# Prompt attention of a hybrid decoder layer: TensorE's order written out by hand, with transposes and value products three steps behind the scores

## The chip, the cores and the metric

The kernel runs on one core of a Trainium2 chip. The metric is the device time of one execution, in microseconds (us). The core has TensorE (PE in the profile: matmuls, with its weight loads, PEld, as a row of their own), VectorE (DVE), ScalarE (ACT), GpSimd (POOL), SyncE (SP, which issues most DMAs here) and the DMA engines. Each engine works through its own instructions in order and waits on semaphores for the others.

## What is computed

The reference is one inference step of a decoder layer over a prompt (2048 tokens) and a group of samples (8 x 8 tokens). Half of the mixing width is softmax attention over three strided windows, merged by their denominators; the other half is an RWKV-7 mixing, and an MLP follows. The change concerns the prompt's attention alone, which the reference states thus (8 heads of 64, blocks of 128 queries):

```python
BRANCHES = ((128, 1), (512, 4), (2048, 16))
...
    for w, d, M, N, band, bias in statics:
        ...
        s = jnp.einsum('bmrhe,bnrhe->bhrmn', qr, kr).astype(f32) * scale + bias[None, :, None]
        ...
        mx = jnp.max(s, -1)
        e = jnp.exp(s - mx[..., None])
        dn = jnp.sum(e, -1)
        o = jnp.einsum('bhrmn,bnrhe->bhrme', e, vr.astype(f32))
    ...
    for mx, dn, o in zip(maxs, dens, outs):
        sc = jnp.exp(mx - mall)
        num = num + sc[..., None] * o
        den = den + sc * dn
    return num / den[..., None]
```

## The kernel before

The program is one long list of stages: norms and the input projection, RWKV mixing, the prompt's attention, the samples' attention, the output projection, the MLP. A tile scheduler takes the instructions as the Python code emits them, chooses an order on each engine, and sets the semaphores. Where the code doesn't fix an order, the scheduler is free to put an instruction earlier or later on its engine than it was emitted.

The prompt's attention works on pairs of heads, p = 0 to 3 (`attention(p, pump, ahead)`), and in each pair on the branches b = 0, 1, 2 and four groups of queries. A group is two steps in b = 0 and 1 and one step in b = 2, so a pair has 8 + 8 + 4 = 20 steps. A step does this for each of the two heads (`ty`):

- scores `sc`: queries against keys, the keys in a high and a low part (`kst`, `klo`). Both heads together are 8 matmuls in b = 0 and 1, nearly all of 256 columns, and 16 of 128 columns in b = 2. The queries `qst` are read in steps of 1, 4 and 16 elements in the three branches.
- on VectorE one operation per block of scores that adds the bias (`bt`) and takes the maximum into `st`, and on ScalarE an exponential into `e`, with its sum into `st`.
- four transposes of `e` into `pt`, which `evac` copies into `pts`: every other copy on ScalarE, the others on VectorE.
- eight value products `o` out of `pts` and the values `vt`; after the last step of a group ScalarE copies `o` into `ob`.

When a pair is through, `merge(p)` is made. It is a generator, and `pump()` moves it on by two of its `yield`s after each step of the next pair. It takes maxima and denominators out of `st` (GpSimd into `zst` and `mv2`, 40 and 8 small matmuls into `sw`), works out a weight for each branch on VectorE and ScalarE (`nall`, `scw`, `dn`, `wh`), stores it (`wD`) and loads it back in another layout (`wrow`); both DMAs go through SP. Twelve matmuls of `wrow` with `wsel` then spread the weights, VectorE multiplies `ob` by them, and GpSimd adds the branches up (VectorE in the last pair, where the merge has no next pair to lie in). The output projection (`pwo`), whose weights `wo` ScalarE and VectorE split out of `raw` at the end of the stage, follows behind the last merge.

Buffers: `e` four, `pts` four, `pt` two, `sc` three, `o` two, `ax` (the merge's, pairs 0 to 2) one, `vt` four.

Of the kernel before, what the change touches and what calls it, by code (L numbers as in the profile page):

```python
# [9 lines left out]
F32 = mybir.dt.float32  # L10
# [161 lines left out]
def _build(ctx, tc, nc, I, O, dbg, upto):  # L172
# [879 lines left out]

    def attention(p, pump, ahead):
# [5 lines left out]
        for b in range(3):  # L1059
# [7 lines left out]
            vt = None  # L1067
            for grp in range(4):
                vp, vt = vt, next_v()
                o = ppo.tile([P, 512], F32, name="o")  # L1070
                for t2 in range(0, 4, 2 if b < 2 else 4):
                    tl = [grp * 4 + t2 + i for i in range(2 if b < 2 else 4)]
                    w = 512 // len(tl)
                    work = []
                    for ty in range(2):
                        kst, klo, qst = K[ty]
                        ps = psc.tile([P, 512], F32, name="sc")
                        e = ae.tile([P, 512], F32, name="e", bufs=4)
                        blocks = []
                        for x, i in enumerate(tl):  # L1080
# [3 lines left out]
                            PE.matmul(ps[:, c0:c0 + n], cols(qst, b, i, False), cols(kst, b, i, both), start=True, stop=False)  # L1084
                            PE.matmul(ps[:, c0:c0 + n], cols(qst, b, i, False), cols(klo, b, i, both), start=False, stop=True)  # L1085
# [3 lines left out]
                            for hb in range(n // P):  # L1089
                                old = n // P - 1 - hb  # L1090
                                if b == 0:
                                    kv = vt[:, i % 4 - old] if i % 4 >= old else vp[:, 3]
                                else:
                                    kv = (vp if old else vt)[:, i % 4]
                                blocks.append((i, kv, c0 + hb * P, hb == 0, hb == n // P - 1))
                        work.append((e, blocks))
                    ptss = []
                    for e, blocks in work:
                        pt = ppt.tile([P, 512], F32, name="pt")
                        pts = at.tile([P, 512], F32, name="pts", bufs=4)  # L1100
                        for y, (i, kv, c0, fst, lst) in enumerate(blocks):
                            PE.transpose(pt[:, y * P:(y + 1) * P], e[:, c0:c0 + P], ident)  # L1102
                        nb = len(blocks)
                        evac(pts[:, :nb * P], pt[:, :nb * P])
                        ptss.append(pts)
                    for y in range(nb):
# [567 lines left out]
```

## Time and profile before

| | us |
|---|---|
| three runs, median (lowest to highest) | 3356.25 (3349.73 to 3358.73) |
| the profiled execution, its own time | 3357.47 |
| its span, first to last instruction | 3355.7 |
| TensorE busy in the span | 3135.5 (93%) |
| TensorE's weight loads busy | 2865.0 (85%) |
| VectorE busy | 2157.2 (64%) |
| ScalarE busy | 1469.2 (44%) |
| GpSimd busy | 976.1 (29%) |
| first score of the prompt's attention | 1207.76 |
| first matmul of the output projection | 1623.21 |

Busy time is the sum of an engine's instructions, without its waits; a share close to 100% over the whole span doesn't say that the engine bounds each stage, so stages are read from windows of the trace. Matmuls overlap in the trace: each row has a start and a modelled end, and the next one starts before that end.

### The profile page before, as it was taken

Reading aid. Unit: us, or ns where it says so; the run is one execution under the profiler, and the core shown is the slowest. Engines: PE = TensorE matmul, PEld = TensorE weight load, DVE = VectorE, ACT = ScalarE, POOL = GpSimd, SP = SyncE. Lnnn points to the kernel's source line nnn. Section 1 sums busy time; section 2 is a strip of 40 time slices with the busy share of each in tenths; the row PEclk is TensorE's granted clock in tenths of the full one; section 3 lists DMA queues with packets and bytes.
Section 4 is the critical chain, followed back from the end, with each engine's and each line's share of the span. In section 5 each row is a group of like instructions: output and inputs, shape, how many; then the busy total and the mean of one; then the engine's idle time right before and its main releaser. Section 6 shows DMA issues by size and latency. Waiting matters only on the chain.

```text
span 3355.7 us, 63761 instructions
## 1 busy us (share of the span) xinstructions
PE 3135.5 (93%) x24214; PEld 2865.0 (85%) x24214; DVE 2157.2 (64%) x4547; ACT 1469.2 (44%) x3497; POOL 976.1 (29%) x1141
## 2 busy tenths in 40 slices
PE   5999899989988979999799689999999999999999
PEld 5876877877787868888688579999899999899999
DVE  4656677677566435656554577676976767967675
ACT  4545566555555446677222233232433323433332
POOL 1003422453044100111000233343533334533332
PEclk9999999999998989999899789999999999999999
DMA  5465575466456383323766322222232222222222
GB/s 169 137 185 149 131 204 158 109 157 178 124 131 178 106 279 117 126 74 90 243 221 235 123 85 89 64 85 64 98 113 64 88 63 86 88 68 84 64 89 73
DMA packets 349144, 418.55 MB, mean 125 GB/s; under 512 B 117252, under 2 KB 210367, under 8 KB 348837
## 3 DMA queue, kind: packets, MB, share of 16 engines
q1 hardware_dynamic: 348836, 414.48, 41.6%
q8 instruction: 190, 3.11, 0.4%
q14 instruction: 118, 0.96, 0.1%
HBM read 325.62 MB, written 93.46 MB: 125 GB/s over the span
## 4 chain that ended last, share of the span: by engine, by line
PE 72%; DMA 9%; DVE 9%; SPq 3%; issue 2%; POOL 2%; ACT 2%; DVEq 0%; POOLq 0%; ACTq 0%
PE pm L1603 20%; PE pm L1557 17%; PE pj L334 7%; PE pwo L1451 5%; PE pj L802 4%; PE o L1109 3%; PE pt L1102 2%; PE sc L1084 2%; PE sc L1085 2%; DVE ml L182 2%; DMA wr<-in_wq 1%; DMA wr<-in_wr 1%; DVE rl L1517 1%; DVE wl L1477 1%; DMA xg<-in_xg 1%
## 5 line engine op out<-in xcount | busy, mean ns | idle before, releaser
L185 ACT ACTIVATE wh<-wr 128x512 fp32r<-128x512 f32 x744 | 463.4, 625 | 818.5 <-PE pm L1603 473.4
L1603 PE MATMUL pm<-fh,wl 128*128 128x352 f32 x1536 | 495.9, 323 | 8.8 <-DVE wl L1477 8.8
L1603 PE MATMUL pm<-fh,wh 128*128 128x352 f32 x1536 | 493.4, 324 | 0.0
L1603 PE MATMUL pm<-fl,wh 128*128 128x352 f32 x1536 | 492.6, 323 | 0.5 <-DVE fl L182 0.5
L1557 PE MATMUL pm<-ml,wh 128*128 128x352 f32 x1344 | 437.0, 325 | 15.1 <-DVE ml L182 15.1
L1557 PE MATMUL pm<-mh,wh 128*128 128x352 f32 x1344 | 438.6, 327 | 9.4 <-ACT mh L185 9.2
L1557 PE MATMUL pm<-mh,wl 128*128 128x352 f32 x1344 | 436.0, 325 | 5.7 <-DVE wl L1477 4.6
L182 DVE TENSOR_TENSOR res<-pm,res 128x352 f32<-128x352 f32 x384 | 198.6, 522 | 287.5 <-PE pm L1603 284.7
L1477 DVE TENSOR_TENSOR wl<-wr,wh 128x512 fp32r<-128x512 f32 x432 | 361.1, 836 | 6.1 <-ACT wh L185 3.5
L1603 PEld LDWEIGHTS pm<-fh,wl 128*128 128x128 f32 x1536 | 290.2, 189 | 9.8 <-DVE wl L1477 9.8
L1603 PEld LDWEIGHTS pm<-fl,wh 128*128 128x128 f32 x1536 | 289.4, 189 | 1.3 <-DVE fl L182 1.1
L1603 PEld LDWEIGHTS pm<-fh,wh 128*128 128x128 f32 x1536 | 289.2, 189 | 0.8 <-ACT fh L185 0.2
L1557 PEld LDWEIGHTS pm<-ml,wh 128*128 128x128 f32 x1344 | 256.5, 191 | 19.1 <-DVE ml L182 19.0
L1557 PEld LDWEIGHTS pm<-mh,wh 128*128 128x128 f32 x1344 | 256.2, 191 | 11.5 <-ACT mh L185 11.5
L1557 PEld LDWEIGHTS pm<-mh,wl 128*128 128x128 f32 x1344 | 255.8, 190 | 8.9 <-DVE wl L1477 7.3
L802 PE MATMUL pj<-wh,nh 128*128 128x256 f32 (+1 forms) x816 | 242.4, 298 | 13.5 <-ACT qn L185 6.7
L802 PE MATMUL pj<-wh,nl 128*128 128x256 f32 (+1 forms) x816 | 241.1, 296 | 2.2 <-DVE nl L182 2.2
L334 PE MATMUL pj<-nh,wh 128*128 128x512 f32 (+3 forms) x600 | 222.8, 374 | 20.4 <-ACT nh L185 10.4
L1481 POOL TENSOR_TENSOR wr<-wr 128x512 f32<-128x512 f32 x48 | 68.9, 1435 | 591.0 <-DVE wl L1477 502.6
L802 PE MATMUL pj<-wl,nh 128*128 128x256 f32 (+1 forms) x816 | 240.7, 296 | 0.0
L182 DVE TENSOR_TENSOR wl<-wr,wh 128x512 fp32r<-128x512 f32 (+1 forms) x216 | 150.2, 698 | 135.2 <-ACT wh L185 130.0
L334 PE MATMUL pj<-nl,wh 128*128 128x512 f32 (+3 forms) x600 | 222.0, 371 | 5.9 <-DVE nl L182 5.9
(312 smaller groups left out, 7262.2 us busy)
## 6 DMA issues: line engine op xcount, KB each, us to landing
wr<-in_w SPq DMA_DIRECT2D x384, 256.0 KB
wr<-in_wr SPq DMA_DIRECT2D x120, 256.0 KB
wr<-in_wq SPq DMA_DIRECT2D x96, 256.0 KB
kv<-in_kc SPq DMA_DIRECT2D x40, 512.0 KB
kv<-in_vc SPq DMA_DIRECT2D x40, 512.0 KB
xsD<-xst SPq DMA_DIRECT2D x56, 256.0 KB
xrkv<-xsD SPq DMA_DIRECT2D x32, 384.0 KB
vt<-vD SPq DMA_DIRECT2D x48, 256.0 KB
```

The source lines that it names most:

```text
L182: V.tensor_tensor(out, a, b, op)
L185: S.activation(out, in_, func, bias=bias, scale=scale, **kw)
L334: PE.matmul(ps[:m, :n], a[:, k, :m], b[h * 4 + k][:, c0:c0 + n], start=(h == 0 and i == 0), stop=(h == 1 and i == 11))
L802: PE.matmul(out, a[h * 2 + k][:, i * P:i * P + m], b[:, k, :], start=(h == 0 and q == 0 and i % 2 == 0), stop=(h == 3 and q == 5 and (i % ...
L1084: PE.matmul(ps[:, c0:c0 + n], cols(qst, b, i, False), cols(kst, b, i, both), start=True, stop=False)
L1085: PE.matmul(ps[:, c0:c0 + n], cols(qst, b, i, False), cols(klo, b, i, both), start=False, stop=True)
L1109: PE.matmul(o[ty * 64:ty * 64 + 64, (i % 4) * P:(i % 4 + 1) * P], kv[:, ty * 64:ty * 64 + 64], ptss[ty][:, y * P:(y + 1) * P], start=fst, ...
L1451: PE.matmul(ps[:, :NC_], a[k][:, o * P:(o + 1) * P], b, start=(i == 0), stop=(i == 3 * KT - 1))
L1477: (G if pooled else V).tensor_tensor(wl, w, wh.bitcast(F32), ALU.subtract)
L1481: G.tensor_tensor(S[0], A21, A22, ALU.add)
L1557: PE.matmul(ps, a[:, k], b[:, k], start=(n == 0), stop=(n == 11))
L1603: PE.matmul(ps, a[:, f], b[:, cs], start=(i == 0), stop=(i == 11))
```

## The change

It fixes TensorE's order in the attention. Every matmul and transpose of the scores, value products and merge is registered to stay in program order, and the program order is made a line of steps: step k first does the transposes of step k-3 (`turn`), then its own scores, then the value products of step k-3 (`finish`). At the end of the last pair the line is emptied. `e` gets six buffers for four, every fourth copy of transposes goes to ScalarE for every second, the merge is moved on by one `yield` at two places of a step for two at one, and between the load of `wrow` and its first matmul stand four `yield`s for two (one in the last pair).

```diff
-        if evac.n % 2 in (0,):
+        if evac.n % 4 == 0:
...
+    def mul(*a, **k):
+        tc.keep_in_program_order(PE.matmul(*a, **k))
+
+    def turned(*a, **k):
+        tc.keep_in_program_order(PE.transpose(*a, **k))
...
+    def finish(step):
+
+        b, grp, ob, first, last, work, ptss = step
...
+        for y in range(len(work[0][1])):
+            for ty in range(2):
...
+                mul(o[ty * 64:ty * 64 + 64, (i % 4) * P:(i % 4 + 1) * P], kv[:, ty * 64:ty * 64 + 64], ptss[ty][:, y * P:(y + 1) * P], start=fst, stop=lst, tile_position=(0, ty * 64))
+        if not last:
+            return
+        if b == 0:
+            act(ob[:, grp * 512:(grp + 1) * 512], o, AF.Copy)
...
+    def turn(step):
+
+        for e, blocks in step[5]:
+            pt = ppt.tile([P, 512], F32, name="pt")
+            pts = at.tile([P, 512], F32, name="pts", bufs=4)
+            for y, (i, old, c0, fst, lst) in enumerate(blocks):
+                turned(pt[:, y * P:(y + 1) * P], e[:, c0:c0 + P], ident)
+            nb = len(blocks)
+            evac(pts[:, :nb * P], pt[:, :nb * P])
+            step[6].append(pts)
...
+                for t2 in range(0, 4, nt_):
+                    back = line.pop(0) if len(line) == LAG else None
+                    if back:
+                        turn(back)
+                    pump()
...
-                        e = ae.tile([P, 512], F32, name="e", bufs=4)
+                        e = ae.tile([P, 512], F32, name="e", bufs=2 * LAG)
...
+                    line.append((b, grp, ob[b], t2 == 0, t2 + nt_ == 4, work, []))
+                    if back:
+                        finish(back)
                     pump()
                     next(coming, None)
...
+        while p == 3 and line:
+            back = line.pop(0)
+            turn(back)
+            finish(back)
         return merge(p, ob, st)
+
+    LAG = 3
...
-        yield
-        yield
+        for _ in range(4 if p < 3 else 1):
+            yield
...
         def pump():
-            for _ in range(2):
-                next(before, None)
+            next(before, None)
```

The PE.matmul calls of scores and merge become `mul` calls with the same operands. In TensorE's order the three kinds of a step stood mixed before, in the stage 683 runs of one kind; now there are 281 runs, with the same number of matmuls of each kind.

First place, TensorE inside the first branch of pair 1: the steps around the first matmul of pair 0's weights (`ax<-wrow,wsel`). Before, it stood here, in the first steps of the second branch (the scores of 128 columns are that branch's first group):

```order
L1109 MATMUL o<-pts,vt 64x128 x7
L1102 MATMUL pt<-ident,e 128x128 x4
L1084 MATMUL sc<-kst_15178,qst_15180 128x128
L1085 MATMUL sc<-klo_15179,qst_15180 128x128
L1109 MATMUL o<-pts,vt 64x128
L1102 MATMUL pt<-ident,e 128x128 x4
L1197 MATMUL ax<-wrow,wsel 128x512
L1084 MATMUL sc<-kst_15175,qst_15177 128x128
```

Now it stands in the first branch. Behind the eight small matmuls on `mv` come three steps (the last of them is shown, from its transposes to its value products), one more group of transposes, and then it:

```order
L1057 MATMUL pt<-ident,e 128x128 x8
L1054 MATMUL sc<-kst_15104,qst_15106 128x256
L1054 MATMUL sc<-klo_15105,qst_15106 128x256
L1054 MATMUL sc<-kst_15104,qst_15106 128x256
L1054 MATMUL sc<-klo_15105,qst_15106 128x256
L1054 MATMUL sc<-kst_15107,qst_15109 128x256
L1054 MATMUL sc<-klo_15108,qst_15109 128x256
L1054 MATMUL sc<-kst_15107,qst_15109 128x256
L1054 MATMUL sc<-klo_15108,qst_15109 128x256
L1054 MATMUL o<-pts,vt 64x128 x8
L1057 MATMUL pt<-ident,e 128x128 x8
L1054 MATMUL ax<-wrow,wsel 128x512
```

What moved: the kinds stand in blocks of eight, and the matmul on `wrow` stands 32 rows of the list behind the last small matmul for 85 before.

Second place, TensorE at the end of pair 3, from the last scores to the products of the last weights with `wsel`. Before (`sc<-mcon,zst` and `sc<-mv_14820,mcon` are the merge's 32 and 8 small matmuls, `sc<-kv,qbd` belongs to the samples' attention):

```order
L1102 MATMUL pt<-ident,e 128x128
L1146 MATMUL sc<-mcon,zst 32x32 x10
L1102 MATMUL pt<-ident,e 128x128
L1146 MATMUL sc<-mcon,zst 32x32 x12
L1102 MATMUL pt<-ident,e 128x128
L1152 MATMUL sc<-mv_14820,mcon 32x256 x8
L1109 MATMUL o<-pts,vt 64x128 x7
L1102 MATMUL pt<-ident,e 128x128 x4
L1109 MATMUL o<-pts,vt 64x128 x8
L1257 MATMUL sc<-kv,qbd 32x256 x8
L1197 MATMUL sc<-wrow,wsel 128x512 x12
```

Now:

```order
L1054 MATMUL o<-pts,vt 64x128 x8
L1057 MATMUL pt<-ident,e 128x128 x8
L1054 MATMUL o<-pts,vt 64x128 x8
L1057 MATMUL pt<-ident,e 128x128 x8
L1054 MATMUL o<-pts,vt 64x128 x8
L1057 MATMUL pt<-ident,e 128x128 x8
L1054 MATMUL o<-pts,vt 64x128 x8
L1054 MATMUL sc<-ident,st 32x128 x8
L1054 MATMUL sc<-mcon,zst 32x32 x32
L1054 MATMUL sc<-mv_14820,mcon 32x256 x8
L1289 MATMUL sc<-kv,qbd 32x256 x8
L1054 MATMUL sc<-wrow,wsel 128x512 x12
```

What moved: the small matmuls of the merge stand behind all transposes and value products of the last three steps, where they stood between the last transposes and the last 15 value products.

Third place, ScalarE at the same end of pair 3, from the output weights' copies (`wo<-raw`) to the merge's exponential (`scw<-scw`). Before:

```order
L185 ACTIVATE pts<-pt 128x512
L185 ACTIVATE sw<-sc 128x512
L185 ACTIVATE wo<-raw 128x512 x2
L185 ACTIVATE sw<-sc 128x256
L185 ACTIVATE wo<-raw 128x512
L185 ACTIVATE ob_18007<-o 128x128x4
L185 ACTIVATE pts<-pt 128x512
L185 ACTIVATE wo<-raw 128x512
L185 ACTIVATE scw<-scw 128x384
L185 ACTIVATE ob_18007<-o 128x128x4
L185 ACTIVATE wo<-raw 128x512 x3
L185 ACTIVATE wh_19245<-scw 128x384
```

Now:

```order
L185 ACTIVATE wo<-raw 128x512 x2
L185 ACTIVATE pts<-pt 128x512
L185 ACTIVATE wo<-raw 128x512
L185 ACTIVATE ob_17929<-o 128x128x4
L185 ACTIVATE wo<-raw 128x512 x3
L185 ACTIVATE ob_17929<-o 128x128x4
L185 ACTIVATE pts<-pt 128x512
L185 ACTIVATE ob_17929<-o 128x128x4
L185 ACTIVATE sw<-sc 128x512
L185 ACTIVATE sw<-sc 128x256
```

What moved: the last copies of transposes (`pts`) and of value products (`ob`), and with them both copies of the merge's `sw`, stand behind the last of the twelve copies of the output weights; before, `sw` stood behind three and five of them, and six came behind the last `pts`.

In SP's list the 24 loads of the keys and queries of pair 0 all stand behind the last stores of the projection, the load of `wsel` ahead of them; before, twelve of them stood ahead of the last of those stores, and the load of `wsel` behind all 24.

## Rows read from the trace of the kernel before

**Rows 1.** Windows: from:to, length, busy us of PE, PEld, DVE, ACT, POOL; clock; DMA share, GB/s.
```profile
1245.00:1309.00 64.00, 64.00 (x477) 53.65 (x478) 29.17 (x145) 42.02 (x149) 1.17 (x4) 0.97 0.21 67
1309.00:1405.00 96.00, 95.49 (x766) 79.29 (x767) 56.33 (x237) 65.66 (x227) 12.92 (x16) 0.99 0.37 123
1405.00:1496.50 91.50, 91.16 (x751) 77.37 (x750) 56.22 (x240) 65.52 (x229) 12.76 (x16) 0.98 0.38 126
1496.50:1591.00 94.50, 93.61 (x735) 78.89 (x734) 61.25 (x254) 70.28 (x245) 17.76 (x28) 0.98 0.34 92
```

**Rows 2.** Timeline of TensorE, first branch: start, length, line, operation, tiles, count, [idle before].
```profile
1412.69 0.28 PE L1084 MATMUL sc<-kst,qst 128*128 128x256 f32 x1
1412.81 0.28 PE L1085 MATMUL sc<-klo,qst 128*128 128x256 f32 x1
1413.01 0.33 PE L1109 MATMUL o<-pts,vt 128*64 128x128 f32 x2
```

**Rows 3.** Timeline of TensorE, second branch of the first pair.
```profile
1264.72 0.43 PE L1109 MATMUL o<-pts,vt 128*64 128x128 f32 x2
1265.08 0.66 PE L1102 MATMUL pt<-ident,e 128*128 128x128 f32 x4
1265.49 0.58 PE L1084 MATMUL sc<-kst,qst 128*128 128x256 f32 x1
1265.89 0.42 PE L1085 MATMUL sc<-klo,qst 128*128 128x256 f32 x1
1266.12 0.42 PE L1084 MATMUL sc<-kst,qst 128*128 128x256 f32 x1
```

**Rows 4.** Timeline of TensorE, third branch of the second pair.
```profile
1384.78 0.39 PE L1084 MATMUL sc<-kst,qst 128*128 128x128 f32 x1
1384.99 0.39 PE L1085 MATMUL sc<-klo,qst 128*128 128x128 f32 x1
...
1385.88 1.09 PE L1109 MATMUL o<-pts,vt 128*64 128x128 f32 x16
1386.91 0.98 PE L1102 MATMUL pt<-ident,e 128*128 128x128 f32 x7
```

**Rows 5.** Timeline of TensorE, merge of the second pair inside the third.
```profile
1409.79 1.08 PE L1152 MATMUL ax<-mv,mcon 128*32 128x256 f32 x14
...
1435.38 0.48 PE L1197 MATMUL ax<-wrow,wsel 128*128 128x512 f32 x1
```

**Rows 6.** Timeline of SyncE's queue, the same merge: issues of its store and load.
```profile
1425.52 1.33 SPq L1187 DMA_DIRECT2D wD<-wh  x4
...
1431.62 0.72 SPq L1190 DMA_DIRECT2D wrow<-wD  x2
```

**Rows 7.** Window of that merge, columns as in the first group.
```profile
1410.00:1436.00 26.00, 26.00 (x243) 20.84 (x235) 18.67 (x75) 21.57 (x72) 0.00 (x0) 1.00 0.78 270
```

**Rows 8.** Timeline of TensorE, the tail of the stage.
```profile
1589.99 0.39 PE L1085 MATMUL sc<-klo,qst 128*128 128x128 f32 x1
...
1593.26 1.09 PE L1152 MATMUL sc<-mv,mcon 128*32 128x256 f32 x14 [0.19 <-POOL mv L1133]
...
1613.27 3.54 PE L1197 MATMUL sc<-wrow,wsel 128*128 128x512 f32 x6 [13.37 <-DMA wrow<-wD]
...
1623.21 0.66 PE L1451 MATMUL pwo<-mh,wo 128*128 128x352 f32 x1 [0.40 <-DVE ob L182]
```

**Rows 9.** Timeline of SyncE's queue, the tail's store.
```profile
1605.58 1.33 SPq L1187 DMA_DIRECT2D wD<-wh  x4
```

**Rows 10.** Windows in and behind the tail's wait.
```profile
1605.00:1613.20 8.20, 0.00 (x0) 0.00 (x0) 1.94 (x4) 1.26 (x2) 0.00 (x0) 0.51 0.46 150
1623.30:1628.00 4.70, 4.70 (x16) 4.70 (x17) 4.47 (x11) 1.38 (x3) 0.00 (x0) 0.50 0.31 112
```

**Rows 11.** Timeline of ScalarE, the tail: last copies of the output weights.
```profile
1607.39 1.33 ACT L185 ACTIVATE wo<-raw 128x512 fp32r<-128x512 f32 x2 [2.62 <-DMA raw<-in_wo]
```

**Rows 12.** Timeline of TensorE, the start of the stage.
```profile
1212.67 0.55 PE L1084 MATMUL sc<-kst,qst 128*128 128x256 f32 x1 [2.65 <-DMA qst<-qD]
```

More of the change, by code (lines that the diff above doesn't have):

```diff
@@ L1066, in attention @@
                     ahead["bias", p + 1, b - 1] = bias_load(p + 1, b - 1)
-            vt = None
             for grp in range(4):
[L1069 to L1072, printed above, removed]
+                nt_ = 2 if b < 2 else 4
+                for t2 in range(0, 4, nt_):
[3 more added lines that the diff above has]
+                    pump()
+                    tl = [grp * 4 + t2 + i for i in range(nt_)]
                     w = 512 // len(tl)
@@ L1089, in attention @@
                             for hb in range(n // P):
[L1090 to L1095, printed above, removed]
-                        work.append((e, blocks))
[L1097 to L1106, printed above, removed]
-                        for ty in range(2):
-                            i, kv, c0, fst, lst = work[ty][1][y]
-                            PE.matmul(o[ty * 64:ty * 64 + 64, (i % 4) * P:(i % 4 + 1) * P], kv[:, ty * 64:ty * 64 + 64], ptss[ty][:, y * P:(y + 1) * P], start=fst, stop=lst, tile_position=(0, ty * 64))
+                                blocks.append((i, n // P - 1 - hb, c0 + hb * P, hb == 0, hb == n // P - 1))
+                        work.append((e, blocks))
+                    line.append((b, grp, ob[b], t2 == 0, t2 + nt_ == 4, work, []))
+                    if back:
+                        finish(back)
                     pump()
                     next(coming, None)
-                if b == 0:
-                    act(ob[b][:, grp * 512:(grp + 1) * 512], o, AF.Copy)
-                elif b == 1:
-                    act(ob[b][:, grp * 512:(grp + 1) * 512].rearrange("p (n q) -> p n q", q=4), o.rearrange("p (q n) -> p n q", q=4), AF.Copy)
-                else:
-                    act(ob[b].rearrange("p (m r) -> p m r", r=16)[:, :, grp * 4:(grp + 1) * 4], o.rearrange("p (r m) -> p m r", r=4), AF.Copy)
         for _ in coming:
@@ L1140, in merge @@
                 c0 = x * 96 + g * 8
-                PE.matmul(ps[32 * g:32 * g + 32, x * P:x * P + P], flat[:, c0:c0 + 32], ident, start=True, stop=True, tile_position=(0, 32 * g))
+                mul(ps[32 * g:32 * g + 32, x * P:x * P + P], flat[:, c0:c0 + 32], ident, start=True, stop=True, tile_position=(0, 32 * g))
         for x in range(2):
@@ L1145, in merge @@
                     c0 = 256 + x * P + q * 32
-                    PE.matmul(ps[32 * g:32 * g + 32, c0:c0 + 32], zst[:, x, q, g], rr1, start=True, stop=True, tile_position=(0, 32 * g))
+                    mul(ps[32 * g:32 * g + 32, c0:c0 + 32], zst[:, x, q, g], rr1, start=True, stop=True, tile_position=(0, 32 * g))
         act(sw[:, 0:4].rearrange("p a n -> p (a n)"), ps, AF.Copy)
@@ L1151, in merge @@
             for ty in range(2):
-                PE.matmul(ps[32 * g:32 * g + 32, 0:256], d2[:, g, ty], mv2[:, ty].rearrange("p x g c m -> p (x g c m)"), start=(ty == 0), stop=(ty == 1), tile_position=(0, 32 * g))
+                mul(ps[32 * g:32 * g + 32, 0:256], d2[:, g, ty], mv2[:, ty].rearrange("p x g c m -> p (x g c m)"), start=(ty == 0), stop=(ty == 1), tile_position=(0, 32 * g))
         act(sw[:, 4:6].rearrange("p a n -> p (a n)"), ps[:, 0:256], AF.Copy)
@@ L1196, in merge @@
                 ps = mp()
-                PE.matmul(ps, wsel[:, g], wr[:, b], start=True, stop=True)
+                mul(ps, wsel[:, g], wr[:, b], start=True, stop=True)
                 tt(ob[b][:, cs], ps, ob[b][:, cs], ALU.mult)
```

19 lines of the change are left out of this document (17 added, 2 removed).

## Prediction

> **What bounds the kernel now.** I first read the table of windows over the prompt-attention stage [rows 1]. The reader is to see two things in it, apart from where it lies. The change touches only this stage. From 1245 to 1591 TensorE is busy almost without a break (64.00 of 64, 95.49 of 96, 91.16 of 91.5, 93.61 of 94.5) while VectorE and ScalarE stand at 56 to 70 us per pair. And the same arithmetic takes 64 us for two branches of the first pair and 91.5 to 96 for three branches of each later one, so a pair is now some 94 us of TensorE.
>
> Then I read the starts in TensorE's timeline, because the modelled ends of matmuls overlap and only the distance from one start to the next is a cost. In a long run a score of the first branch costs 0.12 (1412.69 to 1412.81), and going over to the value products 0.20 [rows 2]. In the second branch a score costs 0.23, a transpose 0.10 (four in 0.41), and two records of value products standing alone 0.36 before the next kind starts [rows 3]. In the third a score costs 0.21, and sixteen records of value products together 1.03 [rows 4], 0.13 a pair. So a pair of value products alone costs nearly three times what it costs in a run. TensorE is the bound here, but part of its time is switching.
>
> Last I followed the merge of the pair before, which runs inside the next pair: its last small matmuls (on mv) run from 1409.79 for some 1.02 us, and the first matmul on the weights (wrow) starts at 1435.38 [rows 5], 24.6 us behind them. Between them stand a chain of small operations on VectorE and ScalarE, a store at 1425.52 and a load at 1431.62 [rows 6]. TensorE never waited for that: from 1410 to 1436 it was busy all 26.00 us [rows 7]. Only in the tail, with no scores left, it stood 13.37 us for the same load [rows 8].
>
> **The change, part by part.** Durations come from the profiled execution: 3357.47 us, a span of 3355.7 and 1.8 around it; that is 1.2 us above the median of the runs (3356.25). The sum is made against 3357.5.
>
> *Fixed runs.* A step is now eight transposes, its scores, eight value products, all of one kind together. From the rows above it costs TensorE in the first branch 0.8 + 1.0 + 1.0 = 2.8 us [rows 2 to 4], in the second 0.8 + (8 x 0.23 + 0.1) + 1.0 = 3.7, in the third 0.8 + (16 x 0.21 + 0.1) + 1.0 = 5.3. Eight, eight and four steps are 22.4, 29.9 and 21.3, together 73.6. The merge adds 12 wrow matmuls of 0.48 each (5.8 us, [rows 5]) and 48 small ones, which I put at 3 by the 14 that took 1.02; with 2 us for what doesn't fit, 84.5 for a pair, if nothing waits.
>
> The first pair has no merge in it. At 1245 eight of its scores' steps are issued, so 1245 to 1309 is branches two and three: 29.9 + 21.3 and little else, 52 against 64 us. **Term 1: -12.** Bounds: -15 by the starts alone, 0 if the switches are not real (third rival).
>
> *VectorE takes three of four copies of transposes instead of one of two.* Of the 160 copies (two per step) 40 move from ScalarE, 10 per pair. VectorE is at 56 to 61 of 91 to 96 us [rows 1], and a copy is about 0.6, so a pair has room for the 6 us. It lies beside TensorE and costs nothing except in the first branch, where VectorE has the merge's chain too; I price that below.
>
> *The wrow matmul in a fixed place.* This is the part that decides. Before, the scheduler put it 25 us behind the small matmuls, into the second branch. Now three steps and one group of transposes stand between: 3 x 2.8 + 0.8 = 9.2 us of work for TensorE, 13 when VectorE stretches these steps with the chain. In order, everything behind (scores, transposes, value products of all later steps) waits with it, and VectorE and ScalarE wait for those. How long the way from mv to wrow becomes no row shows, for TensorE has not stood still there. From below: the tail, where nothing competes but copies of the output weights, needs from 1594.28 (1593.26 + 1.02) to 1613.27, that is 19.0, of it 7.7 from the store at 1605.58 [rows 9] to the matmul; without the copies it would be some 2 less. From above: the 24.6 of the merge above. I take 19, the tail's, because the stalled TensorE sends VectorE nothing else. So TensorE stands 6 us at each of three pairs, after a stretched 13.
>
> *The clock after a stall.* In the tail the granted clock was 0.51 over 1605 to 1613.2, in TensorE's wait, and 0.50 over 1623.3 to 1628, when it worked again [rows 10]; that is the lower level, 1.2 GHz. The first five microseconds of work cost some 2.4 that way. I take 2 per pair, part of it under VectorE. The Trainium skill (TensorE: Matmul & The Clock Gate, HAM oscillation — how this bites in real kernels) says that a wait inside a loop which is long enough puts TensorE back to its lower clock each time, so the transition is paid per pass. Our tail agrees once (0.50 after the stand); no row of before shows it inside the pairs. By that rule each pair pays its 2 us; without it the sum would be 6 us lower.
>
> A pair, then: 7.3 to the last small matmul (two steps and 48 matmuls), 19 to wrow, 2 for the clock, 11 for the last three steps of the first branch with six wrow matmuls, 29.9 + 2.8 for the second branch with the other six, 21.3 for the third: 93.3. Three of them are 280 against 96 + 91.5 + 94.5 = 282 [rows 1]. **Term 2: -2.** Bounds: 84.5 each (-28) and 100 each (+18).
>
> *The drain at the end.* After the last scores (1589.99, [rows 8]) the small matmuls came at once, and mv at 1593.26. Now three steps of transposes and value products go first, each 0.8 + 1.0 and some 1.1 for the copy between, which has no scores over it any more: 8.7 us if copies are immediate. They are not: on ScalarE all twelve copies of the output weights stand ahead of the last such copy, and they are paced by loads; in the trace the last two ended at 1608.7 (1607.39 + 1.33) after a wait of 2.62 [rows 11]. Freed of the chain I take the twelfth at about 1604. Then 2 us to the last value products, 4 for the 48 small matmuls, 7 for a chain that has VectorE to itself, 7.7 from the store to the first matmul and 10 for the twelve products (1613.27 to 1623.21, [rows 8]): 1635 against 1623.2. **Term 3: +12**, bounds +6 (copies not in the way) and +16.
>
> *The start.* In the new order all loads of K and Q for the first pair are issued behind the last projection stores; before, a few went earlier. TensorE already waited 2.65 for one at 1212.67 [rows 12]. Against that, the load for wsel goes out earlier, so ScalarE no longer stops among its exponentials. I take **Term 4: -1**, between -5 and +4. Four to six e buffers and the yields are at nothing: no instruction is added.
>
> Sum: -12 - 2 + 12 - 1 = -3, so 3357.5 - 3 = 3354 us. About 0.3% (10 us) can be told from no change in this kernel.
>
> **The rivals.** *Faster: nothing waits.* If the weights come back within some 11 us of the small matmuls, or if TensorE had more air than its starts show, pairs cost 84.5, and the sum is -12 - 28 + 12 - 1 = -29: 3328 us. For it speaks that a chain on a free VectorE is short; against it, that 7.7 us are the store and load alone. A sentence of the skill points the same way: the Trainium skill (Perfetto Trace Analysis, Identifying the Most-Contended Engine) calls matmul busy share a poor measure and takes weight loads' busy share. Here that is 79.29 of 96 against 95.49 [rows 1], and 16 us of room in a pair would be about 80, beyond even this rival. The rows agree that the matmul share hides room; whether the order gets at it is open.
>
> *Slower: the weights' round trip at the head of the line.* If VectorE and ScalarE, still full of other work, need the same 24.6 us, each pair stands 12 us and costs 99; with a drain of +14 the sum is -12 + 15 + 14 - 1 = +16: 3373. It decides from about 23.5 us between mv and wrow. For it: the first branch is where VectorE is densest, 18.67 of 26 us [rows 7], and it gets more copies. Against: its other work runs dry when TensorE stands.
>
> *Absorbed.* Steps are set by the way from scores through VectorE, ScalarE and the copy back, not by TensorE's switches: the first pair saves 3, pairs stay at 94, the drain costs 12: 3366. Against: the three steps of lag are 8 to 11 us, and the busy shares.
>
> **How the numbers follow.** Forecast 0.45 (3344 to 3364; of it 0.10 below 3346 and 0.02 above 3366), nothing waits 0.27, round trip 0.20, absorbed 0.08 (half of it slower). Faster 0.10 + 0.27 = 0.37; slower 0.02 + 0.20 + 0.04 = 0.26; same 0.37. The likeliest case's own range is 3344 to 3364; with the upper half of the first rival and the lower part of the second the range is 3328 to 3374.
>
> **What would show it.** Branches two and three of the first pair in about 52 us, with eight transposes, scores and value products each in one run. TensorE idle once per later pair, about 6 us, released by the load of wrow, and a granted clock under 0.9 behind it. Pairs of about 93 us. In the tail, value products waiting for copies on ScalarE, and the first product with the output weights some 45 us behind the last score. Wrong would be: no wait at wrow (first rival), a wait of 10 us or more (second), or many short waits of transposes and value products for copies (third).

## The result and the profile after

The changed kernel takes 3609.31 us (median of 4 runs, 3604.3 to 3614.02) against 3354.12 for the kernel before on the same chip: a ratio of 1.076, with an interval from 1.0739 to 1.0782. That is 255 us slower. The forecast was 3354, its range ended at 3374.

The windows of the stage, pair by pair and then the tail (from:to, length, busy us of PE, PEld, DVE, ACT, POOL; clock; DMA share, GB/s), answer to [rows 1]:

```profile
1216.80:1356.70 139.90, 109.27 (x579) 88.93 (x579) 51.99 (x219) 62.03 (x209) 2.80 (x8) 0.68 0.33 113
1356.70:1513.40 156.70, 122.80 (x752) 98.53 (x751) 65.86 (x250) 66.85 (x218) 13.00 (x16) 0.70 0.22 74
1513.40:1673.80 160.40, 127.06 (x753) 102.25 (x751) 66.22 (x250) 66.88 (x218) 15.57 (x19) 0.67 0.20 65
1673.80:1834.30 160.50, 123.88 (x728) 99.32 (x726) 71.26 (x258) 70.38 (x224) 13.60 (x22) 0.67 0.20 55
1834.30:1877.40 43.10, 24.06 (x215) 16.03 (x214) 25.61 (x49) 11.38 (x23) 1.41 (x2) 0.62 0.32 101
```

A pair takes 157 to 160 us where it took 91.5 to 96. TensorE, before almost without a gap, is busy for some 125 of them, VectorE and ScalarE for 66 to 71. Nothing is full any more, and the granted clock is 0.67 to 0.70 for 0.98 to 0.99. The profile's span grew by 252.6 us, and from the starts in the two timelines this divides without a rest: the first score comes 9.1 later (1216.89 for 1207.76), the way from the first to the last score grew from 382.2 to 617.3 (+235.1), the tail behind it from 33.2 to 43.1 (+9.9), and the rest of the program is 1.5 shorter.

The list of what TensorE waited for in the stage (total us, times, longest) names it:

```profile
PE sc L1054 <- DVE st L1134: 134.3, 224, 2.3
PE sc L1054 <- DMA wrow<-wD: 12.4, 1, 12.4
PE sc L1054 <- DMA qst<-qD: 10.1, 1, 10.1
```

The wait for `wrow` lies in the tail and that for `qst` ahead of the first score; what is left is 134.3 us in 224 waits of scores for VectorE's reading of scores (`st`). The number can be counted in the code: in the first two branches a head's score tile holds two blocks, so one wait for each head and step, 2 x 16 steps; in the third it holds four, so three waits, 6 x 4 steps; 56 a pair, 224 in all. Every block that isn't the first of its tile waits. In the listing of TensorE's order with its semaphores it stands so (`DVE_49` is VectorE's):

```
L1054 MATMUL sc<-kst_15104,qst_15106 128x256
L1054 MATMUL sc<-klo_15105,qst_15106 128x256
L1054 MATMUL sc<-kst_15104,qst_15106 128x256 [waits DVE_49]
L1054 MATMUL sc<-klo_15105,qst_15106 128x256
```

The timeline of TensorE in pair 2, one step of the second branch and the start of the third (start, length, line, operation, tiles, count, [idle before]):

```profile
1460.40 0.56 PE L1054 MATMUL sc<-kst,qst 128*128 128x256 f32 x1
1460.78 0.41 PE L1054 MATMUL sc<-klo,qst 128*128 128x256 f32 x1
1461.87 0.60 PE L1054 MATMUL sc<-kst,qst 128*128 128x256 f32 x1 [0.67 <-DVE st L1134]
1462.29 0.42 PE L1054 MATMUL sc<-klo,qst 128*128 128x256 f32 x1
1462.53 0.42 PE L1054 MATMUL sc<-kst,qst 128*128 128x256 f32 x1
1462.76 0.42 PE L1054 MATMUL sc<-klo,qst 128*128 128x256 f32 x1
1463.81 0.60 PE L1054 MATMUL sc<-kst,qst 128*128 128x256 f32 x1 [0.63 <-DVE st L1134]
1464.24 0.41 PE L1054 MATMUL sc<-klo,qst 128*128 128x256 f32 x1
1464.58 1.97 PE L1054 MATMUL o<-pts,vt 128*64 128x128 f32 x16
1466.48 1.73 PE L1057 MATMUL pt<-ident,e 128*128 128x128 f32 x8
1467.97 0.44 PE L1054 MATMUL sc<-kst,qst 128*128 128x128 f32 x1
1468.24 0.39 PE L1054 MATMUL sc<-klo,qst 128*128 128x128 f32 x1
1469.12 0.48 PE L1054 MATMUL sc<-kst,qst 128*128 128x128 f32 x1 [0.49 <-DVE st L1134]
```

The reader is to see the step from 1460.78 to 1461.87: the second block of head 0 starts 1.47 behind the first (1460.40), where the prediction counted two scores at 0.23. VectorE's rows at that place show what lies between:

```profile
1460.78 0.69 DVE L1005 COPY pts<-pt 128x512 f32<-128x512 f32 x1 [0.16 <-PE pt L1057]
1461.39 0.41 DVE L1134 CUSTOM_DVE_ANT_0 e<-sc,bt 128x256 f32<-128x256 f32 x1
```

VectorE is on a copy of transposes when the first block is done, reads the block from 1461.39 to 1461.80, and at 1461.87 TensorE goes on. In the third branch one block to the next is 1.15 (1467.97 to 1469.12) for 0.42. The products and transposes behind such waits take nearly twice as long: sixteen records of value products 1.90 (1464.58 to 1466.48) for 1.03 in [rows 4], eight transposes 1.49 (1466.48 to 1467.97) for 0.8. The granted clock over these products is 0.50, the lower of its two levels (columns as in the windows above):

```profile
1464.58:1466.48 1.90, 1.90 (x17) 1.57 (x16) 0.43 (x2) 0.60 (x2) 0.59 (x2) 0.50 0.25 66
```

Scores with no wait between them (1462.29, 1462.53, 1462.76) follow at 0.24 and 0.23, as before.

### The profile page after: what moved, and what is told of

Same layout as the page of the kernel before. It is cut to its first block, busy times and chain, and to the rows that moved or that the text cites. A ratio compares the mean times of both kernels' runs of the same rounds, so it can differ in the third digit from the quotient of the medians.

```text
span 3608.3 us, 63799 instructions
## 1 busy us (share of the span) xinstructions
PE 3254.7 (90%) x24214; PEld 2949.5 (82%) x24214; DVE 2195.9 (61%) x4587; ACT 1476.0 (41%) x3457; POOL 976.3 (27%) x1141
## 4 chain that ended last, share of the span: by engine, by line
PE 70%; DVE 11%; DMA 8%; issue 4%; SPq 3%; POOL 2%; ACT 2%; DVEq 0%; POOLq 0%; ACTq 0%
PE pm L1634 19%; PE pm L1588 16%; PE pj L334 7%; PE pwo L1482 5%; PE sc L1054 5%; PE pj L802 4%; PE o L1054 3%; PE pt L1057 2%; DVE e L1134 2%; DVE ml L182 1%; DMA wr<-in_wq 1%; DMA wr<-in_wr 1%; PE pu L658 1%; DVE rl L1548 1%; DMA mt<-mtd 1%
## 5 line engine op out<-in xcount | busy, mean ns | idle before, releaser
L1054 PE MATMUL sc<-kst,qst 128*128 128x256 f32 (+1 forms) x384 | 176.0, 461 | 144.5 <-DVE st L1134 134.3
L185 ACT ACTIVATE e<-e,st 128x256 f32<-128x256 f32 (+1 forms) x384 | 176.7, 460 | 233.0 <-DVE st L1134 231.0
L1134 DVE CUSTOM_DVE_ANT_0 e<-sc,bt 128x256 f32<-128x256 f32 (+1 forms) x384 | 138.3, 365 | 216.9 <-PE sc L1054 208.2
L1588 PEld LDWEIGHTS pm<-ml,wh 128*128 128x128 f32 x1344 | 256.3, 191 | 16.8 <-DVE ml L182 16.8
L1054 PEld LDWEIGHTS sc<-kst,qst 128*128 128x128 f32 x384 | 109.0, 284 | 193.5 <-DVE st L1134 182.7
```

The costliest lines, as they stand in the source:

```text
L185: S.activation(out, in_, func, bias=bias, scale=scale, **kw)
L1054: tc.keep_in_program_order(PE.matmul(*a, **k))
L1134: V.tensor_tensor_reduce(out=e[:, c0:c0 + n], in0=ps[:, c0:c0 + n], in1=bts[ty][:, 256 - n:256], scale=-1.0, scalar=3e38, op0=ALU.add, op1 ...
L1588: PE.matmul(ps, a[:, k], b[:, k], start=(n == 0), stop=(n == 11))
```

## The experiments

**Theory.** The two or four blocks of a step and head are parts of one score tile in PSUM, the memory that these matmuls write to. The semaphores in the listing let no matmul write a block there while VectorE still has to read the block ahead of it. The free order put other work into that time: in the listing of the kernel before, 2 to 91 other matmuls and transposes stand between such a block and the one ahead of it in its tile, 14 in the median. The fixed one puts the block directly behind, in all 224 cases. The waits then lower TensorE's clock, and the half clock makes the rest of the loss. The Trainium skill (PSUM — Partial Sum Buffer, PSUM bank collisions raise a hardware error) says that two engines must not access one bank and quadrant of PSUM at once, and that the compiler's scheduler adds a dependency between any two instructions of different engines that touch the same one; the 224 waits agree with it. Whether the semaphores here go by the tile or by the bank no run separates. **Rival.** The order of the three kinds in itself, with three of four copies on VectorE, makes VectorE and ScalarE too slow for TensorE.

All times from starts in TensorE's timelines of the profiled executions: the first score; the way from first score to first score of the next pair (of pair 3: to the last score); and from there to the first product with the output weights. The last column is the median of the runs; a profiled execution can lie some us off it (10 with the merge in the drain). The first score also holds how long the unchanged stages ahead of it took: the last store of the projection (`klD`) went out between 1192.0 and 1207.3. From that store to the first score it is 5.0 before, 5.4 with a line of two, and 16.8 to 18.0 in all the others:

| kernel | first score | pair 0 | pair 1 | pair 2 | pair 3 | tail | time |
|---|---|---|---|---|---|---|---|
| before | 1207.8 | 104.7 | 93.4 | 91.6 | 92.6 | 33.2 | 3354 to 3356 |
| after | 1216.9 | 139.8 | 156.8 | 160.4 | 160.4 | 43.1 | 3609.31 |
| heads alternate | 1218.3 | 94.5 | 109.8 | 109.6 | 116.3 | 41.3 | 3424.5 |
| products between | 1218.9 | 84.6 | 99.3 | 102.0 | 105.5 | 44.7 | 3389.22 |
| tile per block | 1218.7 | 85.2 | 102.8 | 98.9 | 101.6 | 40.4 | 3380.3 |
| waits filled | 1224.2 | 122.9 | 132.0 | 132.3 | 137.1 | 38.0 | 3519.21 |
| nothing fixed | 1216.8 | 93.6 | 93.0 | 99.1 | 96.9 | 31.9 | 3361.53 |
| weights later | 1216.6 | 86.4 | 95.4 | 94.5 | 96.7 | 40.5 | 3362.43 |
| line of two | 1211.0 | 97.8 | 102.4 | 102.4 | 105.7 | 38.2 | 3388.83 |
| merge in the drain | 1209.2 | 83.7 | 102.5 | 98.7 | 102.7 | 41.1 | 3382.14 |
| half of the copies | 1221.8 | 83.9 | 89.2 | 91.6 | 91.1 | 40.7 | 3353.7 |
| free tail | 1221.1 | 86.6 | 95.4 | 94.8 | 96.4 | 36.8 | 3360.14 |
| third branch mixed | 1222.3 | 84.9 | 96.3 | 95.6 | 103.8 | 32.8 | 3365.73 |
| all repairs | 1215.1 | 83.1 | 92.0 | 92.2 | 100.2 | 32.0 | 3348.14 |

**Heads alternate.** The blocks of the two heads are emitted by turn.

```diff
-                    for ty in range(2):
...
-                        for x, i in enumerate(tl):
+                    for x, i in enumerate(tl):
+                        for ty in range(2):
```

> The changed kernel with one edit: the score blocks of a step are emitted head by turn (first block of head 0, first of head 1, second of head 0, ...) instead of all blocks of a head together; nothing else. Theory 1 (a score matmul must wait until VectorE has read the block ahead of it in the same PSUM tile, and in a fixed order nothing else can go ahead): the other head's two matmuls now lie in each wait, so the 134 us of waits of scores on VectorE fall to 30 to 75 us, the granted clock of the stage rises from 0.66-0.71 to 0.8 or more, and the time falls to 3400-3500. Theory 2 (the order of transposes, scores and value products with three of four copies on VectorE makes VectorE and ScalarE too slow for TensorE): no more than 30 us away from 3609.

Measured: 3424.5 us, one run; the granted clock from the first to the last score is 0.87 for 0.68. Of the 134.3 us the profile keeps:

```profile
PE sc L1054 <- DVE st L1133: 30.1, 70, 1.2
```

185 us of the 255 go with the order of eight matmuls inside a step, while copies, line and yields stay. The theory's numbers hold, the waits at the lower end of their range; the rival's don't.

**Value products between the blocks.** As above, and the value products of three steps back stand behind the first blocks.

```diff
+                        if fill:
+                            fill.pop(0)()
...
-                    if back:
-                        finish(back)
+                    while fill:
+                        fill.pop(0)()
```

> As heads alternate, and the eight value products of three steps back stand between the score blocks (in the third branch four behind the first and four behind the second block) instead of behind all of them. Theory 1: nearly every wait is covered by work that was ready anyway; waits of scores on VectorE under 25 us, clock 0.95 or more until 1600, time 3320-3390, and only now the wait for wrow at each pair can show (6 us each by the forecast). Theory 2: within 30 us of 3609, since the copies and their engines are the same.

Measured: 3389.22 us, 1.0103 [1.0073, 1.0132] against before. The scores' wait for VectorE is gone from the list, and the wait that the prediction was about comes into it:

```profile
PE ax L1054 <- DMA wrow<-wD: 26.3, 3, 11.5
```

The time is at the upper end of what was expected, and the clock of 0.95 or more did not come: it is 0.91 from the first to the last score, 0.81 to 0.88 in the first branches and 1.00, 0.96, 0.84 and 0.72 in the third ones.

**A tile per block.** No order changes, only the tile into which a block is written.

```diff
-                        ps = psc.tile([P, 512], F32, name="sc")
...
+                            ps = psc.tile([P, 512], F32, name="sc")
-                            mul(ps[:, c0:c0 + n], cols(qst, b, i, False), cols(kst, b, i, both), start=True, stop=False)
+                            mul(ps[:, :n], cols(qst, b, i, False), cols(kst, b, i, both), start=True, stop=False)
```

> The changed kernel with one edit: each score block gets a PSUM tile of its own out of the same three (psc), so that a matmul waits for VectorE's reading of the block three back and not of the one just before. TensorE's order, the line of three steps and the copies stay. Theory 1: the 224 waits shrink from 0.6 us to 0.2 or nothing, scores' waits on VectorE under 40 us, the clock back to 0.9 or more, time 3340-3430. Theory 2: within 30 us of 3609.

Measured: 3380.3 us, 1.0079 [1.0049, 1.0109]. The waits:

```profile
PE ax L1054 <- DMA wrow<-wD: 19.0, 3, 10.2
...
PE sc L1054 <- DVE st L1134: 13.7, 27, 1.0
```

The sequence of kinds on TensorE is that of the changed kernel, and 229 us of the 255 are gone; so it was the shared tile, not the sequence. The waits of scores for VectorE that are left lie nearly all in first branches, where scores follow at 0.12 and the fourth block of a step needs the first of the three tiles again. The clock from the first to the last score is 0.90, at the edge of what was expected. A step of pair 0's second branch in its timeline:

```profile
1254.87 1.09 PE L1057 MATMUL pt<-ident,e 128*128 128x128 f32 x8
1255.71 0.58 PE L1054 MATMUL sc<-kst,qst 128*128 128x256 f32 x1
1256.11 0.42 PE L1054 MATMUL sc<-klo,qst 128*128 128x256 f32 x1
1256.35 0.42 PE L1054 MATMUL sc<-kst,qst 128*128 128x256 f32 x1
...
1257.94 1.09 PE L1054 MATMUL o<-pts,vt 128*64 128x128 f32 x16
1258.96 0.66 PE L1057 MATMUL pt<-ident,e 128*128 128x128 f32 x4
```

0.84 for the transposes, 2.23 for the scores, 1.02 for the value products, with no idle: 4.09 (3.85 in the mean of this branch's eight steps), against the 3.7 forecast and the 7.1 of the changed kernel (57.0 for the eight steps of pair 2's second branch).

**Waits filled.** Transposes of the identity that nothing reads stand in the waits; the score tiles are two for three.

```diff
+                            if x + 1 < len(tl):
+                                for z in range(DUM):
+                                    turned(jnk[:, z % 4 * P:z % 4 * P + P], ident, ident)
```

> The changed kernel with five transposes of the identity into an unused PSUM tile in front of each score block that isn't the first of its tile (1120 in all, work that nothing reads; the score tiles go from three to two to make room). If the clock is what makes the 134 us of waits cost 255 (theory 1 with the clock): TensorE is kept busy in the waits, the granted clock of the stage goes back above 0.9, and although work is added the time FALLS by 90 to 150 us, to 3460-3520. If the clock plays no part (the waits, or the engines behind them, make the whole loss): within 40 us of 3609, or above it.

Measured: 3519.21 us, one run: 90 us faster with 1120 more transposes. Windows of its pairs 1 and 2, columns as above:

```profile
1347.00:1479.00 132.00, 125.18 (x1032) 105.96 (x1031) 65.03 (x250) 66.49 (x218) 13.00 (x16) 1.00 0.26 89
1479.00:1611.00 132.00, 125.08 (x1030) 105.69 (x1029) 65.02 (x249) 66.27 (x219) 13.48 (x15) 1.00 0.24 79
```

The clock is 1.00 where it was 0.70 and 0.67, and a pair takes 132 where it took 157 to 160. So the waits lower the clock. Part of them is left:

```profile
PE sc L1056 <- DVE st L1136: 22.9, 46, 4.2
```

What the clock cost can be estimated from this one run. The added transposes follow each other at 0.11, so the 280 of a pair are some 31 us, and 6 us of waits are left in it (22.9 / 4); without both a pair would take some 95. A tile per block comes to the same: 101, of which 6 are its wait for `wrow`. So of some 64 us that a pair lost to the shared tile (159 less 95), 33 (134.3 / 4) were waits and the rest, some 30, is put down to the half clock; over the four pairs some 120 of the 255. The timeline above gives the same size: products and transposes together 1.5 longer a step, 20 steps a pair.

**Nothing fixed.** `mul` and `turned` are plain matmul and transpose, all other edits stay.

```diff
-        tc.keep_in_program_order(PE.matmul(*a, **k))
+        PE.matmul(*a, **k)
...
-        tc.keep_in_program_order(PE.transpose(*a, **k))
+        PE.transpose(*a, **k)
```

> The changed kernel with only the fixing taken back: no matmul is held in program order; the line of three steps, six e buffers, the copies (three of four on VectorE), the yields and the drain stay as emission order, from which the scheduler is free to depart. Theory 1 (a fixed order exposes the waits within a score tile): the scheduler puts other work into these waits again, scores' waits on VectorE under 5 us, and the time is 3345-3375, the start some 9 us later than before because the first loads of K and Q still stand behind the projection's stores. Theory 2 (copies or the line cost the time): above 3450.

Measured: 3361.53 us, 1.0024 [1.0006, 1.0041]. The wait at the score tiles:

```profile
PE sc L1054 <- DVE st L1134: 0.4, 1, 0.4
```

All other edits together cost some 8 us (2 to 14 by the interval); the fixed order cost the rest. The late start is not what these 8 us are: the first score comes 9.0 later, but pair 0 is 11.1 shorter and ends 2.1 earlier than before. Pairs 2 and 3 are 7.5 and 4.3 longer, with third branches of 35.0 and 32.7 for 29.4 and 28.9; no run shows why.

**Weights two steps later.** From here on the runs build on a tile per block; each expectation says on which.

```diff
-        for _ in range(4 if p < 3 else 1):
+        for _ in range(8 if p < 3 else 1):
```

> On top of a tile per block: eight yields for four between the load of wrow and its first matmul, so that in TensorE's fixed order it stands two steps (about 6 us) farther back in each of pairs 1 to 3; nothing else. If the wait at the head of the line (19.0 us in three waits with a tile per block) is what keeps that kernel above the one before: those waits fall to 0-6 us, the first branches of pairs 1 to 3 from 41, 41 and 48 us to 34-38, and the time from 3380 to 3350-3368. If the first branch is bound by VectorE's work instead, the waits only move: within 8 us of 3380.

Measured: 3362.43 us, 1.0026 [1.0015, 1.0038]. The wait for `wrow` in the pairs is gone (19.0 with a tile per block), the first branches take 32.6, 33.6 and 39.1, and 18 us are won. What is left there is VectorE; all but 0.6 of this lies in first branches:

```profile
PE sc L1054 <- DVE st L1134: 16.4, 25, 3.7
```

**A line of two.**

```diff
-    LAG = 3
+    LAG = 2
```

> On top of a tile per block: LAG = 2, so e has four buffers again as before the change, and the loads of K and Q of the first pair go back to where they were in SP's order. If the six e buffers (another placement in memory, so that those loads wait for the projection's end) are what delays the start: the first score goes from 1218.7 back to 1208-1211, and the time falls by 6 to 11 us to 3368-3375, if two steps of lag cover the way through VectorE and ScalarE; if they don't, many short waits of transposes on e appear and the time stays or rises.

Measured: 3388.83 us, 1.0097 [1.0068, 1.0126]. The loads of K and Q went back to their place in SP's order and the first score came at 1211.0, 5.4 behind the last store, as expected. But pair 0's first branch then took 39.3 and ended 44.7 behind that store, against 47.2 with a tile per block and 42.6 before: most of the 12 us was gone by then. The time was not won, and the waits of scores on VectorE rose to 19.3 from 13.7. Waits of transposes on `e`, the sign named for a lag that is too short, are not in the list.

**The last merge in the drain.**

```diff
+        rest = merge(p, ob, st)
+        ahead_of = [2, 1, 1]
         while p == 3 and line:
             back = line.pop(0)
             turn(back)
             finish(back)
-        return merge(p, ob, st)
+            for _ in range(ahead_of.pop(0)):
+                next(rest)
+        return rest
```

> On top of a tile per block: in the last pair the small matmuls of the merge are emitted between the three drained steps (40 behind the second, 8 behind the third's transposes and products), not behind all; nothing else. If their place behind the drain sets the tail: the last score to the first product of the output weights goes from 40.4 to 36-39 us and the time by as much, to 3376-3379. If the copies on ScalarE and the store and load of the weights set it: no change within 2 us.

Measured: 3382.14 us, 1.0084 [1.0054, 1.0114], tail 41.1 for 40.4. No gain: moving the 48 matmuls alone doesn't shorten the tail; the last of them still ended 18.3 behind the last score.

**Half of the copies on ScalarE.**

```diff
-        if evac.n % 4 == 0:
+        if evac.n % 2 == 0:
```

> On top of the weights two steps later (3362 us): every second copy of transposes on ScalarE again instead of every fourth. If VectorE's load sets the first branches (33, 34 and 39 us there against 28 before the change): they fall by 1.5 to 4 us each and the time to 3350-3358. If the copies cost nothing where they are, as the prediction had it: within 4 us of 3362.

Measured: 3353.7 us, 0.9988 [0.9974, 1.0002]. First branches 31.1, 31.3 and 35.6 for 32.6, 33.6 and 39.1. The copies moved to VectorE cost some 9 us as soon as TensorE was no longer held by the tiles.

**Free tail.**

```diff
+        i = PE.matmul(*a, **k)
+        if not loose:
+            tc.keep_in_program_order(i)
...
+        if p == 3:
+            loose.append(p)
```

> On top of the weights two steps later: from the last scores of the last pair on nothing is held in program order (the drained transposes and value products and the last merge), all else as there. If the fixed order of drain and merge is what makes the tail 40.5 us for 33.2 before the change (term 3): the tail goes to 32-35 us and the time to 3354-3357. If it is the copies on ScalarE in their own order: no change within 3 us.

Measured: 3360.14 us, 1.0003 [0.9987, 1.0018]; tail 36.8 for 40.5. The tail got half of what was expected, and the time isn't clear of that without the edit; in the next two kernels, which keep it, the tail is 32.8 and 32.0, and it was 31.9 with nothing fixed, about as before the change (33.2).

**Third branch mixed.** Two things at once in the third branch: heads by turn, and the value products in halves.

```diff
+                            fill = [lambda: finish(back, list(range(nb_ // 2))), lambda: finish(back, list(range(nb_ // 2, nb_)))]
```

> The free tail, with the third branch's scores emitted head by turn and the value products of three steps back in two halves behind the first and second pairs of blocks; all else as there. If runs of 16 scores, which load slowly, are what lowers the clock to 0.75-0.88 in third branches without any wait: the clock there goes above 0.92, third branches from 25-28 to 23-25.5 us, and the time to 3342-3351. If the clock is lower for another reason: third branches cost 1 us more for the added switches, 3356-3360.

Measured: 3365.73 us, 1.0023 [1.0008, 1.0038]. The clock in the third branches of pairs 0 and 1:

```profile
1280.00:1303.00 23.00, 23.00 (x155) 20.89 (x151) 11.71 (x60) 14.67 (x59) 0.85 (x4) 0.85 0.17 47
1372.00:1397.00 25.00, 25.00 (x154) 22.83 (x155) 12.98 (x64) 15.18 (x60) 1.14 (x4) 0.82 0.19 53
```

0.85 and 0.82, short of the 0.92 expected, and nothing was won: the four third branches take 25.6, 27.5, 27.3 and 27.6, for 27.5, 28.0, 24.8 and 22.4 with the free tail. The time lies above what either reading expected. Runs of 16 scores are not the cause, or not alone.

**All repairs together.**

> All of these together: a tile per block, weights two steps later, the free tail, third branch mixed, and half of the copies on ScalarE. If all the causes are as read: 3335-3350, faster than the kernel before the change (3355). If VectorE's share plays no part: as the run with the third branch mixed, within 4 us.

Measured: 3348.14 us, 0.9976 [0.9961, 0.999], the fastest of all and faster than the kernel before by 0.24%, 0.1 to 0.4% by the interval. A fixed order with a lag of three can be made to pay, but only a little. This kernel holds the mixed third branch too, which didn't pay by itself; no run has the other repairs together without it.

## Why the prediction was wrong

The step that failed is *Fixed runs*: "A step is now eight transposes, its scores, eight value products, all of one kind together", with 2.8, 3.7 and 5.3 us for it in the three branches. The 0.12, 0.23 and 0.21 a score were read where the scheduler had chosen the order, with every block's tile already read. It was taken for granted that eight scores follow each other at that distance in any order. They don't where the next one goes into the tile of the one before: 7.1 us a step in the second branch, 11.4 in the third (45.4 / 4). The new order's listing with semaphores shows the 224 places where TensorE waits for VectorE in the middle of a run; the prediction looked at the sequence alone.

*Term 1* (-12, branches two and three of pair 0 in 52 us): measured 100.9 (55.6 + 45.3). With a tile per block they take 56.0 (30.8 + 25.2), where from first score to first score they took 67.0 (38.2 + 28.8) before: 11.0 less. With nothing fixed they take 66.1 (36.0 + 30.1), so the saving belongs to the order: it was right in kind and size, and hidden under the tiles.

*Term 2* (-2; wait for wrow of 6 us at each later pair): in the changed kernel there was no such wait in the pairs, because the steps ahead of it took 18.0 to 23.6 us. With a tile per block it comes, 19.0 us in three, with 17.1, 17.0 and 22.9 from the last small matmul to `wrow` for the 19 taken: 6.3 in the mean, as forecast, but 4.4, 4.4 and 10.2 one by one. Pairs 1 to 3 are then 303.3 together against 280 forecast: first branches of 40.8, 41.1 and 47.6 for 39.3, and third branches of 21.3 to 27.9 for 21.3.

*The copies*, costed at nothing, are 9 us in the repaired kernel; VectorE has room in a pair, but less in its first branch, where the merge's chain, the copies and the scores' reading meet: there the waits of scores for it fall from 16.4 to 7.5 when copies go back to ScalarE.

*The clock* was priced at 2 us a pair behind one stall. The many short waits lowered it for the whole stage, which is some 30 us a pair by the estimate from the run with waits filled. None of the 224 waits is longer than 2.3 us.

*Term 3* (+12): measured +9.9. In parts, the last small matmul of the merge ended 18.1 behind the last score (20 forecast, 4.4 before), the first matmul on `wrow` came 13.2 later (14.7 forecast, 18.9 before), and the output projection 11.7 behind that (10 forecast, 9.9 before). The copies stand on ScalarE where the prediction saw them; these are rows of ScalarE's timeline in the changed kernel's drain, and one of TensorE's:

```profile
1840.21 0.63 ACT L185 ACTIVATE wo<-raw 128x512 fp32r<-128x512 f32 x1 [0.82 <-DMA raw<-in_wo]
1840.74 0.58 ACT L185 ACTIVATE pts<-pt 128x512 f32<-128x512 f32 x1
...
1841.38 1.97 PE L1054 MATMUL o<-pts,vt 128*64 128x128 f32 x14 [1.80 <-ACT pts L185]
...
1845.76 0.63 ACT L185 ACTIVATE wo<-raw 128x512 fp32r<-128x512 f32 x1 [0.74 <-DMA raw<-in_wo]
1847.47 0.60 ACT L185 ACTIVATE ob<-o 128x512 f32<-128x512 f32 x1 [1.08 <-PE o L1054]
1848.56 0.60 ACT L185 ACTIVATE pts<-pt 128x512 f32<-128x512 f32 x1 [0.48 <-PE pt L1057]
```

The copy at 1840.74 comes behind output weights that waited for their load, and TensorE's products wait 1.80 for it, as the prediction had it. The last copy (1848.56) also comes behind the last of the output weights (1845.76), but waits in the end for TensorE's transposes, 0.48, not for that one. So the size of the term came out nearly, its reason only in part. With nothing fixed the last small matmul ends 3.7 behind the last score and the tail is 31.9; the three kernels with a free tail have 36.8, 32.8 and 32.0. So the fixed order of the drain makes it; which part of that order wasn't taken apart.

*Term 4* (-1): from the last store of the projection the first score came 12 us later (17.3 for 5.0), but the end of pair 0's first branch 0.5 to 4.6 later in the kernels with a tile per block (43.1 to 47.2 for 42.6). So the late loads cost little by then.

*The rivals*: the third, "Steps are set by the way from scores through VectorE, ScalarE and the copy back", was nearest, and the prediction put against it that three steps of lag cover that way. They do; what no lag covers is the way inside one step, from a block through VectorE to the next block of its tile.

## What to carry to other kernels

Before fixing an engine's order, take the distance from one start to the next only where the same neighbours stand side by side; for a new neighbourhood list the waits of the new order, and see how much other work stands between an instruction and the one that it waits behind. Two blocks in one PSUM tile were a chain here through the engine that reads them: give each its own tile, or put other work of TensorE between. 56 short waits a pair cost their own length here, 33 us, and by estimate nearly as much again by the clock.

## What the runs showed of the hardware beyond that

The granted clock also fell where TensorE's rows show no wait at all. In the run with the weights two steps later, pair 1's second branch, the first six microseconds of its third, and the whole third:

```profile
1336.00:1371.00 35.00, 34.07 (x243) 29.53 (x243) 24.50 (x86) 19.86 (x73) 10.60 (x12) 1.00 0.20 63
1371.00:1374.00 3.00, 3.00 (x16) 2.90 (x18) 2.10 (x14) 2.77 (x14) 0.00 (x0) 1.00 0.00 0
1374.00:1377.00 3.00, 3.00 (x23) 2.67 (x24) 0.54 (x3) 1.46 (x6) 0.00 (x0) 0.54 0.20 53
1371.00:1398.00 27.00, 27.00 (x155) 25.24 (x156) 12.62 (x69) 16.10 (x69) 1.62 (x4) 0.75 0.23 71
```

TensorE is busy 27.00 of 27, and the clock is 0.75, while the second branch ahead of it, with 34.07 of 35 busy, has 1.00. The third branch's step is then 16 scores of 128 columns at 0.22, and the products behind them take 1.67 (sixteen records, 1373.93 to 1375.60) for 1.02. Before the change the clock of the later pairs was 0.98 to 0.99 [rows 1], but it fell in third branches there too. These are the four, pair by pair, in the trace of the kernel before:

```profile
1283.64:1312.48 28.84, 28.84 (x232) 24.83 (x230) 11.78 (x68) 19.53 (x74) 0.58 (x2) 0.88 0.15 43
1377.06:1405.84 28.78, 28.51 (x280) 25.26 (x278) 13.79 (x71) 19.92 (x74) 3.37 (x5) 1.00 0.22 66
1468.05:1497.42 29.37, 29.10 (x279) 25.92 (x279) 13.62 (x71) 20.22 (x74) 3.52 (x6) 0.94 0.22 64
1561.09:1589.99 28.90, 28.90 (x231) 25.57 (x229) 13.62 (x71) 20.16 (x75) 3.76 (x6) 0.94 0.12 38
```

With a tile per block the four have 0.87, 0.76, 0.86 and 0.92, with the third branch mixed 0.87, 0.78, 0.78 and 0.94. What in the stream decides this stays open. It is not all that kept third branches above the 21.3 us of the forecast: with products between, pair 0's took 24.7 at a clock of 1.00.
